# Elementwise work of GpSimd given to the vector and scalar engines, and the S5 chunk scan as a first-order scan in a rotating frame, in a hybrid encoder layer

## The chip, the cores and the metric

The kernel runs on one core of a Trainium2 chip. The metric is the device time of one execution in microseconds (us). The kernel before takes 930.8 us (median of 3 runs, 930.01 to 931.61).

Five engines work side by side, each on its own queue in program order: PE (TensorE, matmuls), DVE (VectorE), ACT (ScalarE), POOL (GpSimd) and SP (SyncE, which issues most of the DMAs). PEld is the loading of weights into PE. An instruction that waits holds up everything behind it in its own queue.

## What is computed

The reference is one layer of a sequence model: 512 positions, 1024 channels, float32. An RMS norm, one input projection, four causal mixers side by side, a gated merge, an output projection, a squared-ReLU MLP and a final norm.

```python
h = _rmsnorm(x, norm1_g)
proj = h @ w_in
p_gdn, p_lru, p_s5, p_rwkv, p_gate = _split(proj, (...))
ys = (_gdn_mixer(p_gdn, ...), _rglru_mixer(p_lru, ...), _s5_mixer(p_s5, ...), _rwkv7_mixer(p_rwkv, ...))
for i in range(N_BRANCH):
    term = jax.nn.sigmoid(gate_logits[:, :, i]) * (ys[i] @ w_branch[i])
    merged = term if merged is None else merged + term
x = x + merged @ w_out
x = x + jnp.square(jax.nn.relu(_rmsnorm(x, norm2_g) @ mlp_w1)) @ mlp_w2
return _rmsnorm(x, final_norm_g)
```

The S5 mixer is the one whose method is changed. It has 16 groups with 64 complex states each; with `lam_bar = exp(lam * dt)` per group and state it is

```python
bu = jnp.einsum("gpc,bsgc->bsgp", b_bar, ug)
h = _linear_recurrence(lam_bar, bu)          # h_t = lam_bar * h_{t-1} + bu_t
y = jnp.einsum("gcp,bsgp->bsgc", c, h).real + d * ug
```

## The kernel before

**Weights.** All large products go through 134 units of weights, each 128 rows by 1024 columns in float32. `fetch_` (L300) brings a unit in: SP loads `raw`, ACT rounds it to `hi`, DVE takes `lo = raw - hi`. There are two buffers of each (`DEEP = 2`), so unit u needs the buffers of unit u - 2 to be free. `gemm` (L317) multiplies a unit in 24 matmuls of 128x512, three for each of 8 slices: `hi` by the high part of the activation, `hi` by its low part, `lo` by the high part. The third matmul of a unit is therefore the first that needs `lo`.

**Phases.** `norm1` (L389) splits x into `xgh` and `xgl` and takes its rms (`norm_stat`, L325); the projections start before the rms is known, and `nproj` (L402) multiplies it in when it takes a result out of PSUM. 22 units are the mixers' input projections and 32 the gates' (`gate`); the mixers' own work stands between them, up to some 30 units in. Then come the branch products (`branch`, 8 units), the merge (8) and the MLP (`mlp`, L1377, 64 units). The last part is the final norm (L1405).

**S5** works in chunks of 8 positions, 64 chunks. `s5_weights` (L1058) makes `lam_bar` (`er`, `sn`, `cs1`, ...), its powers `pw` and the factors; `s5_a` builds `b8` and `s5_o` builds `c8` and Toeplitz blocks, with two products of 128x2048 and an addition each; `s5_b` gives `H`, each chunk's drive, 128 x (re | im) x 8 groups x 64 chunks; `s5_c` (L1235) carries the state over the chunks: blocks of 8 chunks, complex multiply-adds by powers of `lam_bar^8` (`q8`, `li8`), 22 calls of `cmul_add`, all on GpSimd. Then `H` goes by 4 DMAs to `hs`, PE makes `s5y`, a store and 16 loads (`scy`, issued by ACT) turn it round, two DVE instructions add `d * u`, and the gelu and the `glu` product follow.

**The other mixers.** rwkv and gdn each need a triangular inverse (`tri_inverse`, L425), which passes through DRAM (`scrr`, `scrg`). In rwkv, `hsk`/`hbk` are head sums (`head_stat`, L370), `wl` and `al` lora products, `bkT`, `vT` transposes; in the RG-LRU (`lru`, L1004), `lra` and `lrx` are the gates' products and `tt(G, u, u, i, MUL)` (L1028) is the input `u*i`. `lg` is gdn's logits, `ktT` its transposed keys, `oT` the transposed outputs.

**Order.** The order within each queue is not written out by hand: the steps of `PLAN` (L58) are traced with a priority by level (`LV`, L53) and a scheduler merges them by its own estimates when the kernel is built. So a change of one instruction's engine moves others. SBUF places of temporaries come from `al` (L128), which reads a table made for one order (`PLACE`, L23).

Helpers record most instructions at one line each: L104 matmul, L107 activation, L110 `tt` (a tensor_tensor instruction), L114 and L116 `ts`, L119 `stt` (scalar_tensor_tensor). Names such as `c`, `c1a`, `c1b` in the profile are the SBUF regions, not the temporaries.

## Time and profile before

| | before |
|---|---|
| median of 3 runs | 930.8 us (930.01 to 931.61) |
| the profiled execution's span, first to last instruction | 929.2 us |
| around the span (median less span) | 1.6 us |
| busy: PE, DVE, ACT, POOL | 891.0, 517.2, 336.1, 214.7 us |
| instructions: PE, DVE, ACT, POOL | 5267, 854, 453, 229 |
| mean granted clock of PE | 0.978 |
| DMA traffic | 99.52 MB, mean 107 GB/s |

The profile lists every instruction with start, duration and, in brackets, how long its engine had been idle before and what released it. An instruction that is held while it executes, not before, shows no idle time but a long duration. The clock column is the share of full speed that PE was granted. In a row such as `70.77 0.80 PE L104 MATMUL acc<-c,lo ...` the first number is the start in us from the span's begin, the second the duration of the group; `x2` says how many instructions are in it.

### The profile page before, as it was taken

How to read it: one execution, taken by the hardware profiler on the slowest of the kernel's cores; microseconds unless marked ns; L12 is line 12 of the kernel's file. 1: busy time of each engine (PE TensorE's matmuls, PEld its weight loads, DVE VectorE, ACT ScalarE, POOL GpSimd, SP SyncE). 2: the span in 40 equal slices, each digit the busy share in tenths (PEclk: the TensorE clock that was granted, in tenths of full speed). 3: DMA queues.
4: the chain of work that ended last, by engine and by line, in shares of the span. 5: the costliest groups of instructions: out<-in, count | busy, mean ns of one | idle time of the engine just before them, and what ended most of it. 6: DMA issues, size and time to landing. Idle time of an engine off the chain costs nothing.

```text
span 929.2 us, 13124 instructions
## 1 busy us (share of the span) xinstructions
PE 891.0 (96%) x5267; PEld 715.0 (77%) x5267; DVE 517.2 (56%) x854; ACT 336.1 (36%) x453; POOL 214.7 (23%) x229
## 2 busy tenths in 40 slices
...
GB/s 250 180 47 78 113 49 96 115 104 105 182 161 162 172 111 152 68 92 69 90 91 91 98 107 91 91 91 95 110 91 91 99 105 91 91 107 97 80 80 90
DMA packets 73675, 99.52 MB, mean 107 GB/s; under 512 B 41920, under 2 KB 48768, under 8 KB 73600
## 3 DMA queue, kind: packets, MB, share of 16 engines
...
HBM read 85.44 MB, written 11.08 MB: 104 GB/s over the span
## 4 chain that ended last, share of the span: by engine, by line
PE 84%; DVE 5%; POOL 5%; ACT 3%; issue 1%; DMA 1%; ACTq 0%; SPq 0%; DVEq 0%; POOLq 0%
PE acc L104 26%; PE facc L104 19%; PE dacc L104 19%; PE bacc L104 5%; PE oacc L104 5%; POOL c L110 4%; DVE c L119 2%; PE oT L104 2%; ACT c L107 1%; DVE c L110 1%; POOL c1a L110 1%; PE s5y L104 1%; DVE lo L110 1%; DVE c L1194 1%; ACT L107 1%
## 5 line engine op out<-in xcount | busy, mean ns | idle before, releaser
L104 PE MATMUL acc<-c,hi 128*128 128x512 f32 x864 | 288.7, 409 | 5.0 <-DVE c L119 3.6
L107 ACT ACTIVATE hi<-raw 128x1024 fp32r<-128x1024 f32 x134 | 142.1, 1060 | 401.7 <-issue 157.5
L110 POOL TENSOR_TENSOR c<-c 128x512 f32<-128x512 f32 (+4 forms) x86 | 117.7, 1377 | 430.0 <-ACT c1a L107 240.2
L104 PEld LDWEIGHTS acc<-c,hi 128*128 128x128 f32 x864 | 164.9, 193 | 48.7 <-DVE c L119 7.1
L110 DVE TENSOR_TENSOR lo<-raw,hi 128x1024 fp32r<-128x1024 f32 x134 | 173.1, 1292 | 49.8 <-ACT hi L107 49.1
L104 PE MATMUL acc<-c,lo 128*128 128x512 f32 x432 | 174.2, 404 | 7.1 <-DVE lo L110 7.1
L104 PE MATMUL facc<-c,hi 128*128 128x512 f32 x512 | 157.7, 389 | 0.0
L104 PEld LDWEIGHTS facc<-c,hi 128*128 128x128 f32 x512 | 96.1, 188 | 19.9
L104 PEld LDWEIGHTS acc<-c,lo 128*128 128x128 f32 x432 | 83.6, 193 | 26.1 <-DVE lo L110 7.8
L104 PE MATMUL facc<-c,lo 128*128 128x512 f32 x256 | 99.8, 390 | 0.0
L104 PE MATMUL dacc<-c1a,hi 128*128 128x512 f32 x256 | 99.6, 389 | 0.0
L104 PE MATMUL dacc<-c1b,hi 128*128 128x512 f32 x256 | 98.9, 389 | 0.0
L104 PE MATMUL dacc<-c1a,lo 128*128 128x512 f32 x256 | 98.9, 389 | 0.0
L110 DVE TENSOR_TENSOR c<-dacc,c 128x512 f32<-128x512 f32 x32 | 22.1, 692 | 97.0 <-PE dacc L104 96.5
L107 ACT ACT_TABLE_LOAD x40 | 51.3, 1283 | 17.2 <-issue 5.9
L104 PEld LDWEIGHTS dacc<-c1a,hi 128*128 128x128 f32 x256 | 48.0, 188 | 10.1
L104 PEld LDWEIGHTS facc<-c,lo 128*128 128x128 f32 x256 | 48.1, 188 | 10.0
L104 PEld LDWEIGHTS dacc<-c1b,hi 128*128 128x128 f32 x256 | 48.1, 188 | 9.9
L104 PEld LDWEIGHTS dacc<-c1a,lo 128*128 128x128 f32 x256 | 48.0, 188 | 9.9
L119 DVE SCALAR_TENSOR_TENSOR c<-facc,c 128x512 f32<-128x512 f32 x32 | 21.9, 691 | 54.1 <-PE facc L104 50.9
L107 ACT ACTIVATE c<-c 128x512 f32<-128x512 f32 (+3 forms) x71 | 39.8, 572 | 25.7 <-DVE c L110 9.9
L110 DVE TENSOR_TENSOR c<-acc,c 128x512 f32<-128x512 f32 x27 | 18.6, 689 | 45.7 <-PE acc L104 45.6
...
## 6 DMA issues: line engine op xcount, KB each, us to landing
raw<-in_wall_dram SPq DMA_DIRECT2D x134, 512.0 KB, 3.5
...
```

The costliest lines, as they stand in the source:

```text
L104: P.matmul(out=o, lhsT=l, rhs=r, start=start, stop=stop)
L107: A.activation(out=o, in_=i, func=f, scale=scale, bias=bias)
L110: e.tensor_tensor(out=o, in0=a, in1=b, op=op)
L119: V.scalar_tensor_tensor(out=o, in0=a, scalar=s, in1=b, op0=op0, op1=op1)
L1194: V.tensor_copy(out=q8[64 * e:64 * e + 64, :, 0], in_=pw[64 * e:64 * e + 64, :, 8, e:16:2])
```

## The change

Every GpSimd instruction that reads SBUF goes to another engine; GpSimd keeps its fills. To DVE go: the additions of the norms' squares, products in rwkv's first part (`ea`, `af`, `rf`) and an addition in its last, lru's `u*i`, six of gdn's products and sums (`gr`, `br`, `kx`, `kd`) and one addition in `gdn_c`, the 128x2048 products and additions of `s5_a` and `s5_o`, the 24 merge additions of `branch`, and three products at the end. To ACT go: four squares of the first norm, rwkv's `rb` scaling, gdn's `ksq` squares and some copies. In the MLP ACT squares the ReLU in place and rounds it in a second pass, where ACT had squared and rounded in one and GpSimd had squared again.

The chunk scan of S5 is done in polar form. With `lam_bar^8 = a e^(i w)`, `s5_weights` makes a, cos w and sin w by three squarings and a correction of the length; `s5_o` makes tables `ct`, `st` of cos(w n) and sin(w n) for the 64 chunks by doubling, and `am`, the decay a with 0 at each group's first chunk. `s5_c` turns `H` back by w n, runs a real first-order scan with decay `am` on DVE for the real and the imaginary part (512 wide each, the zeros in `am` part the groups), and turns it forward again. The place table is replaced by one that goes by the temporaries' names (`HOME`).

```diff
-PLACE = [(a, int(b)) for a, b in (e.split(":") for e in """
-    c2:47 c0:0 c0:128 c3:204 c3:64 c3:48 c3:272 c3:244 c3:375 c3:533 c1b:91 c3:202 c1a:94 c3:550 c3:64 c1b:110
...
+HOME = {n: [(a[:a.index(":")], int(a[a.index(":") + 1:])) for a in v.split(",")] for n, v in (e.split("=") for e in """
+    xt0=c1b:0 xgh=c0:0 xgl=c0:128 sqa0=c3:650 sqa1=c3:64 sqa2=c3:333 sqa3=c3:618 sqa4=c3:558 sqa5=c1a:81 sqa6=c3:634
...
-    def norm_stat(xt, nm, first=V, parts=1):
-        """1 / rms of xt over the channels, on all partitions; the sum over the tiles in two parts or one."""
+    def norm_stat(xt, nm, parts=1):
             sq = t2(f"sq{nm}{k}")
-            if k < 4 and first is G:
-                tt(G, sq, xt[k], xt[k], MUL)
-            else:
-                act(sq, xt[k], ACT.Square)
-            if k == 0 or k == 7 or k == 4 and first is G:
+            act(sq, xt[k], ACT.Square)
+            if k == 0 or k == 7:
                 accs.append(sq)
             else:
-                tt(first if k < 4 else V, accs[-1], accs[-1], sq, ADD)
+                tt(V, accs[-1], accs[-1], sq, ADD)
                 fr(sq)
...
-            tt(G, ea, ei, af, MUL)
+            tt(V, ea, ei, af, MUL)
-            tt(G, af, af, kf, MUL)
+            tt(V, af, af, kf, MUL)
-            tt(G, rf, rf, kp, MUL)
+            tt(V, rf, rf, kp, MUL)
-            tt(G, of_, of_, bons[m], ADD)
+            tt(V, of_, of_, bons[m], ADD)
...
-        tt(G, v3(gr, 16), v3(gr, 16), neg, ADD)
-        tt(G, v3(gr, 16), v3(gr, 16), s16(gc).rearrange("p (x o) -> p x o", o=1).to_broadcast([128, 16, 64]), SUB)
+        tt(V, v3(gr, 16), v3(gr, 16), neg, ADD)
+        tt(V, v3(gr, 16), v3(gr, 16), s16(gc).rearrange("p (x o) -> p x o", o=1).to_broadcast([128, 16, 64]), SUB)
-        tt(G, v3(br, 16), v3(br, 16), mgs, MUL)
-        tt(G, br, br, gr, MUL)
+        tt(V, v3(br, 16), v3(br, 16), mgs, MUL)
+        tt(V, br, br, gr, MUL)
-        tt(G, v3(kx, 16), v3(ktok, 16), tb(8), MUL)
-        tt(G, v3(kd, 16), v3(ktok, 16), tb(7), MUL)
+        tt(V, v3(kx, 16), v3(ktok, 16), tb(8), MUL)
+        tt(V, v3(kd, 16), v3(ktok, 16), tb(7), MUL)
-            tt(G, u, u, i, MUL)
+            tt(V, u, u, i, MUL)
...
+    def square(c, s, t, u):
+        tt(V, t, c, c, MUL)
+        tt(V, u, s, s, MUL)
+        stt(s, s, 2.0, c, MUL, MUL)
+        tt(V, c, t, u, SUB)
...
+        V.tensor_copy(out=pol[:, 0], in_=s(er))
+        ts(V, pol[:, 1], s(cs1), 1.0, ADD)
+        V.tensor_copy(out=pol[:, 2], in_=s(sn))
+        for _ in range(3):
+            square(pol[:, 1], pol[:, 2], s(t0), s(u1))
+            tt(V, pol[:, 0], pol[:, 0], pol[:, 0], MUL)
+        tt(V, s(t0), pol[:, 1], pol[:, 1], MUL)
+        tt(V, s(u1), pol[:, 2], pol[:, 2], MUL)
+        tt(V, s(t0), s(t0), s(u1), ADD)
+        ts(V, s(t0), s(t0), -0.5, MUL, 1.5, ADD)
+        tt(V, pol[:, 1], pol[:, 1], s(t0), MUL)
+        tt(V, pol[:, 2], pol[:, 2], s(t0), MUL)
...
-        tt(G, q4(b8), cc(bs), pwr(0, 1), MUL)
+        tt(V, q4(b8), cc(bs), pwr(0, 1), MUL)
         tt(V, q4(tm), cc(bx), pwr(1, 1), MUL)
-        tt(G, b8, b8, tm, ADD)
+        tt(V, b8, b8, tm, ADD)
...
-        tt(G, q4(c8), cc(c1), pwr(0, 0), MUL)
+        tt(V, q4(c8), cc(c1), pwr(0, 0), MUL)
         tt(V, q4(tm), cc(c2), pwr(1, 0), MUL)
-        tt(G, c8, c8, tm, ADD)
+        tt(V, c8, c8, tm, ADD)
...
-        # powers 1..8 of lambda_bar^8, rows (g parity, state); li8 holds -im, +im
-        q8_, li8_ = al("s5q", 128), al("s5qn", 128)
-        q8, li8 = v4(q8_, 2, 8), v4(li8_, 2, 8)
-        tq = sm_.tile([128, 2, 8], F, name="s5tq")
+        fr(tm)
+        ct, st, am = t2("s5ct"), t2("s5st"), t2("s5am")
+        ct3, st3, am3 = v3(ct, 8), v3(st, 8), v3(am, 8)
+        pol = S5["pol"]
+        ph_ = al("s5ph", 32)
+        ph = v3(ph_, 4)
         for e in range(2):
-            V.tensor_copy(out=q8[64 * e:64 * e + 64, :, 0], in_=pw[64 * e:64 * e + 64, :, 8, e:16:2])
-        for j in range(1, 8):
-            a = (j + 1) // 2
-            b = j + 1 - a
...
-            tt(V, q8[:, 1, j], tq[:, 0], tq[:, 1], ADD)
-        ts(V, li8[:, 0], q8[:, 1], -1.0, MUL)
-        V.tensor_copy(out=li8[:, 1], in_=q8[:, 1])
-        fr(tm, *S5["tmps"])
-        S5.update(t8w=t8w, c8=c8, q8=q8, li8=li8, q8_=q8_, li8_=li8_)
+            V.tensor_copy(out=ph[64 * e:64 * e + 64, 0:3], in_=pol[64 * e:64 * e + 64, 0:3, e:16:2])
+        V.tensor_copy(out=am3, in_=bcn(ph[:, 0], 64))
+        V.memset(am3[:, :, 0:1], 0.0)
+        V.memset(ct3[:, :, 0:1], 1.0)
+        V.memset(st3[:, :, 0:1], 0.0)
+        tb_ = t2("s5tb")
+        for k in range(6):
+            n = 1 << k
+            u = tb_[:, 0:8 * n].rearrange("p (g n) -> p g n", g=8)
+            v = tb_[:, 256:256 + 8 * n].rearrange("p (g n) -> p g n", g=8)
+            c, s_ = bcn(ph[:, 1], n), bcn(ph[:, 2], n)
+            lo_, up_ = slice(0, n), slice(n, 2 * n)
+            tt(V, u, st3[:, :, lo_], s_, MUL)
+            tt(V, v, ct3[:, :, lo_], s_, MUL)
+            tt(V, ct3[:, :, up_], ct3[:, :, lo_], c, MUL)
+            tt(V, st3[:, :, up_], st3[:, :, lo_], c, MUL)
+            tt(V, ct3[:, :, up_], ct3[:, :, up_], u, SUB)
+            tt(V, st3[:, :, up_], st3[:, :, up_], v, ADD)
+            if k < 5:
+                square(ph[:, 1], ph[:, 2], ph[:, 3], ph[:, 0])
+        fr(tb_, ph_)
+        fr(*S5["tmps"])
+        S5.update(t8w=t8w, c8=c8, ct=ct, st=st, am=am)
...
+    def bcn(ap, n):
+        return ap.rearrange("p (g o) -> p g o", o=1).to_broadcast([128, 8, n])
...
-        q8, li8, H = (S5[n] for n in ("q8", "li8", "H"))
+        ct, st, am, H = (S5[n] for n in ("ct", "st", "am", "H"))
         S5.update({n + "3": v3(S5[t], 16) for n, t in (("t8", "t8w"), ("c8", "c8"), ("ug", "ug"))})
         S5["upv"] = S5["up"].rearrange("p (m t n) -> p m t n", m=2, t=8)
-        H5 = H.rearrange("p (r g b j) -> p r g b j", r=2, g=8, b=8)
-        tA, tB = t1("s5a"), t1("s5b")
-        def cmul_add(dst, src, j, acc, n):
-            a = tA[:, 0:16 * n].rearrange("p (r g b) -> p r g b", r=2, g=8)
-            b = tB[:, 0:16 * n].rearrange("p (r g b) -> p r g b", r=2, g=8)
-            re = q8[:, 0, j].rearrange("p (r g b) -> p r g b", r=1, b=1).to_broadcast([128, 2, 8, n])
-            tt(G, a, src, re, MUL)
+        ta_, tb_ = t4("s5a"), t4("s5b")
+        ct2 = ct.rearrange("p (o n) -> p o n", o=1).to_broadcast([128, 2, 512])
+        for to in range(2):
+            tt(V, v3(ta_, 2), v3(H, 2), ct2, MUL)
             for r in range(2):
-                im = li8[:, r, j].rearrange("p (g b) -> p g b", b=1).to_broadcast([128, 8, n])
-                tt(G, b[:, r], src[:, 1 - r], im, MUL)
-            tt(G, a, a, b, ADD)
-            tt(G, dst, acc, a, ADD)
-        for j in range(1, 8):
-            cmul_add(H5[:, :, :, :, j], H5[:, :, :, :, j - 1], 0, H5[:, :, :, :, j], 8)
-        cr_ = al("s5cr", 128)
-        cr = v4(cr_, 2, 8)
-        G.memset(cr[:, :, :, 0], 0.0)
-        for b in range(7):
-            cmul_add(cr[:, :, :, b + 1:b + 2], cr[:, :, :, b:b + 1], 7, H5[:, :, :, b, 7:8], 1)
-        for j in range(8):
-            cmul_add(H5[:, :, :, :, j], cr, j, H5[:, :, :, :, j], 8)
-        fr(tA, tB, cr_, S5["q8_"], S5["li8_"])
+                tt(V, tb_[:, 512 * r:512 * r + 512], H[:, 512 - 512 * r:1024 - 512 * r], st, MUL)
+            for r in range(2):
+                sl = slice(512 * r, 512 * r + 512)
+                tt(V, H[:, sl], ta_[:, sl], tb_[:, sl], SUB if r != to else ADD)
+                if not to:
+                    V.tensor_tensor_scan(out=H[:, sl], data0=am, data1=H[:, sl], initial=0.0, op0=MUL, op1=ADD)
+        fr(ta_, tb_, ct, st, am)
...
-                tt(G, mg[m], mg[m], gt, ADD)
+                tt(V, mg[m], mg[m], gt, ADD)
...
-                act(dh[:, m, :], r, ACT.Square)
-                tt(G, r, r, r, MUL)
+                act(r, r, ACT.Square)
+                act(dh[:, m, :], r, ACT.Copy)
...
-                tt(G, hs[k], hs[k], rs, MUL)
+                tt(V, hs[k], hs[k], rs, MUL)
```

How this moves instructions, in the queues as built (before has lines some 7 lower than after, from L104 on):

At the start of the program DVE's queue before held the low parts of x (`c0<-c2,pr,c0`, stt) and few additions of squares (`c3<-c3`), since GpSimd did the other ones:

```order
L110 TENSOR_TENSOR lo0_180<-raw0_181,hi0_183 128x1024
L119 SCALAR_TENSOR_TENSOR c0_75<-c2_78,pr_81,c0_75 128x512 x6
L110 TENSOR_TENSOR c3_79<-c3_79 128x512
L119 SCALAR_TENSOR_TENSOR c0_75<-c2_78,pr_81,c0_75 128x512
L110 TENSOR_TENSOR c3_79<-c3_79 128x512
L119 SCALAR_TENSOR_TENSOR c0_75<-c2_78,pr_81,c0_75 128x512
L116 TENSOR_SCALAR omu_176<-pr_81 128x8
```

and now every addition of squares stands between the low parts; this is the end of the stretch:

```order
L126 SCALAR_TENSOR_TENSOR c0_75<-c1b_77,pr_81,c0_75 128x512
L117 TENSOR_TENSOR c3_79<-c3_79 128x512
L126 SCALAR_TENSOR_TENSOR c0_75<-c1b_77,pr_81,c0_75 128x512
L117 TENSOR_TENSOR c3_79<-c3_79 128x512
L126 SCALAR_TENSOR_TENSOR c0_75<-c1b_77,pr_81,c0_75 128x512
L123 TENSOR_SCALAR omu_176<-pr_81 128x8
L123 TENSOR_SCALAR omu_176<-pr_81 128x2
L117 TENSOR_TENSOR c3_79<-pr_81 128x16
L117 TENSOR_TENSOR c3_79<-c3_79,c1a_76 128x512
L126 SCALAR_TENSOR_TENSOR c0_75<-c1b_77,pr_81,c0_75 128x512
L117 TENSOR_TENSOR c3_79<-c3_79 128x512
L126 SCALAR_TENSOR_TENSOR c0_75<-c1b_77,pr_81,c0_75 128x512
```

The low part of the last tile of x, for which unit 0's last matmuls wait, now has six additions ahead of it in DVE's queue, where two were; the narrow rows are other steps' constants.

DVE's queue around `lo7`, before. `c3<-c2,c1a 128x2048` is one of s5's products, the two copies at L1194 and `s5tq` belong to s5's `c8` and powers, `hstk` and the copy at L378 to rwkv's head norm, on which PE's `hbk` waits:

```order
L110 TENSOR_TENSOR c1a_76<-acc_421,c3_79 128x512
L110 TENSOR_TENSOR c3_79<-c2_78,c1a_76 128x2048
L1194 COPY c3_79<-c1a_76 64x2x8 x2
L110 TENSOR_TENSOR lo7_520<-raw7_521,hi7_523 128x1024
L119 SCALAR_TENSOR_TENSOR c3_79<-c1a_76,pr_81,c3_79 128x511
L110 TENSOR_TENSOR s5tq_1237<-c3_79 128x8 x2
L114 TENSOR_SCALAR hstk_305<-hsk_300 128x8
L110 TENSOR_TENSOR c2_78<-c3_79,c1a_76 128x8x64
L110 TENSOR_TENSOR c3_79<-s5tq_1237 128x8
L547 RECIPROCAL hstk_305<-hstk_305 128x8
L110 TENSOR_TENSOR s5tq_1237<-c3_79 128x8 x2
L378 COPY c1a_76<-hstk_305 128x512
```

and now, one unit on, around `lo8`:

```order
L117 TENSOR_TENSOR c1b_77<-acc_476,c3_79 128x512
L117 TENSOR_TENSOR c3_79<-c2_78,c1a_76 128x2048
L117 TENSOR_TENSOR c1a_76<-c3_79 128x16
L117 TENSOR_TENSOR lo8_711<-raw8_712,hi8_714 128x1024
L126 SCALAR_TENSOR_TENSOR c3_79<-c1b_77,pr_81,c3_79 128x511
L117 TENSOR_TENSOR c3_79<-c1a_76 128x16 x2
L117 TENSOR_TENSOR c3_79<-c1a_76 128x2048
L117 TENSOR_TENSOR c1a_76<-c3_79 128x16
L117 TENSOR_TENSOR c3_79<-acc_519,c3_79 128x512
L117 TENSOR_TENSOR lo9_744<-raw9_745,hi9_747 128x1024
L117 TENSOR_TENSOR c3_79<-c2_78,c1a_76 128x2048
```

Three instructions of 128x2048 stand here, where one did, and the rows of `s5tq` are gone.

Around the loads of s5's output (`scy`), ACT's queue before:

```order
L1283 COPY c3_79<-s5y_1597 128x512
L502 COPY c2_78<-z3pr_1864 32x16x32
L1292 DMA c3_79<-scy_1615 16x8x64 x2
L107 ACTIVATE hi24_2508<-raw24_2506 128x1024
L1292 DMA c3_79<-scy_1615 16x8x64 x7
L107 ACTIVATE hi25_2543<-raw25_2541 128x1024
L1292 DMA c3_79<-scy_1615 16x8x64 x6
L686 COPY c3_79<-oT_2662 128x2x64
L1292 DMA c3_79<-scy_1615 16x8x64
L829 DMA c1a_76<-gscr_1978 64x16x64 x2
```

and now:

```order
L1320 DMA c3_79<-scy_1555 16x8x64 x4
L669 COPY c3_79<-c3_79 64x256
L1320 DMA c3_79<-scy_1555 16x8x64 x6
L688 COPY c3_79<-oT_2602 128x2x64
L1320 DMA c3_79<-scy_1555 16x8x64 x6
L114 ACTIVATE hi28_3061<-raw28_3059 128x1024
L114 ACTIVATE c1b_77<-c1b_77 128x512
L114 ACT_TABLE_LOAD
L114 ACTIVATE c3_79<-c3_79 128x1024
```

DVE's queue at the two stt that add `d * u` to these loads (`c3<-c1a,pr,c3`, L119 before and L126 now), before:

```order
L119 SCALAR_TENSOR_TENSOR c3_79<-c1a_76,pr_81,c3_79 128x512
L110 TENSOR_TENSOR lo25_2540<-raw25_2541,hi25_2543 128x1024
L110 TENSOR_TENSOR c2_78<-vtT_2014,c2_78 64x256 x2
L110 TENSOR_TENSOR c3_79<-sn_2655,c3_79 64x256
L110 TENSOR_TENSOR c3_79<-c3_79,wc_251 64x256
L119 SCALAR_TENSOR_TENSOR c3_79<-c1a_76,pr_81,c3_79 128x512
```

and now:

```order
L126 SCALAR_TENSOR_TENSOR c3_79<-c1a_76,pr_81,c3_79 128x512
L668 COPY c1b_77<-r1_2612 64x256
L117 TENSOR_TENSOR c1b_77<-acc_2513,c3_79 128x512
L126 SCALAR_TENSOR_TENSOR c3_79<-c1a_76,pr_81,c3_79 128x512
L117 TENSOR_TENSOR lo28_3058<-raw28_3059,hi28_3061 128x1024
```

Before, `hi24` and `hi25` stood between the loads, and `lo25` between the two stt; now all 16 loads and both stt stand ahead of `hi28` and `lo28`. The scan itself left GpSimd's queue, which went from 153 rows to 17.

More of the change, by code (lines that the diff above doesn't have):

```diff
@@ L47 @@
+""".split())}
 NU = 134
@@ L119, in stt @@
         V.scalar_tensor_tensor(out=o, in0=a, scalar=s, in1=b, op0=op0, op1=op1)
-    regions, live, clock, live_names = {}, {}, [0], []
+    regions, live, clock, turns = {}, {}, [0], {}
     def region(name, n, dt=F):
@@ L130, in al @@
         g = -(-n // GRAN)
-        k = len(live_names)
-        live_names.append(name)
-        if k < len(PLACE):
-            r, o = PLACE[k]
-        else:
+        k = turns[name] = turns.get(name, -1) + 1
+        r, o = HOME[name][k] if k < len(HOME.get(name, ())) else (None, 0)
+        if r is None or regions[r][3] is not dt or regions[r][1][o:o + g].any():
             best = None
@@ L329, in norm_stat @@
             sq = t2(f"sq{nm}{k}")
-            if k < 4 and first is G:
-                tt(G, sq, xt[k], xt[k], MUL)
-            else:
-                act(sq, xt[k], ACT.Square)
-            if k == 0 or k == 7 or k == 4 and first is G:
+            act(sq, xt[k], ACT.Square)
+            if k == 0 or k == 7:
                 accs.append(sq)
             else:
-                tt(first if k < 4 else V, accs[-1], accs[-1], sq, ADD)
+                tt(V, accs[-1], accs[-1], sq, ADD)
                 fr(sq)
@@ L392, in norm1 @@
             split_g(xs[k], "g1", k, xgh[:, k, :], xgl[:, k, :])
-        N1["rs"] = norm_stat(xs, "a", G)
+        N1["rs"] = norm_stat(xs, "a")
         fr(xt)
```

73 lines of the change are left out of this document (38 added, 35 removed).

## The prediction

> **What bounds the kernel now.** I read the busy shares of the page first, then the windows, then the waits of TensorE and what stands in front of them on the other engines. A line of the page, and the windows (columns: stretch in us, its length, busy time of PE, PEld, DVE, ACT and POOL with counts, granted clock, DMA share, GB/s):
>
> ```profile
> PE 891.0 (96%) x5267; PEld 715.0 (77%) x5267; DVE 517.2 (56%) x854; ACT 336.1 (36%) x453; POOL 214.7 (23%) x229
> 63.10:72.50 9.40, 2.33 (x7) 1.52 (x6) 9.36 (x4) 0.56 (x1) 9.40 (x4) 0.64 0.08 22
> 72.50:79.40 6.90, 2.91 (x7) 1.72 (x6) 6.90 (x4) 0.00 (x0) 6.77 (x2) 0.75 0.12 47
> 79.40:86.20 6.80, 5.33 (x14) 4.22 (x15) 6.66 (x27) 0.72 (x1) 0.00 (x0) 0.50 0.12 36
> 86.20:174.40 88.20, 87.50 (x490) 66.52 (x489) 67.30 (x171) 43.76 (x58) 49.62 (x104) 1.00 0.32 93
> 174.40:185.20 10.80, 5.78 (x19) 4.59 (x18) 5.72 (x7) 10.20 (x14) 5.61 (x12) 0.68 0.60 127
> 230.00:913.00 683.00, 682.91 (x3827) 554.75 (x3826) 335.57 (x450) 215.95 (x284) 108.88 (x76) 1.00 0.32 105
> 492.48 21.76 PE acc L104 x96
> ```
>
> TensorE is the bound, and from 230 to 913 us it never stops (682.91 of 683). There 96 matmuls take 21.76 us, 0.2267 each, so a unit of 24 takes 5.44. The matmuls stay the same, so only time in which TensorE waits or runs at a lower clock can be won: before 230 us and after 913. In order of time:
>
> ```profile
> 21.62 0.73 PE L104 MATMUL acc<-c,hi 128*128 128x512 f32 x2 [0.45 <-ACT hi L107]
> 70.77 0.80 PE L104 MATMUL acc<-c,lo 128*128 128x512 f32 x1 [7.07 <-DVE lo L110]
> 80.87 1.11 PE L381 MATMUL hbk<-cs,c1a 128*128 128x128 f32 x4 [5.46 <-DVE c1a L378]
> 179.84 1.97 PE L641 MATMUL bkT<-cs,c 128*128 128x128 f32 x8 [5.02 <-ACT c L642]
> 181.45 1.20 PE L104 MATMUL acc<-c,hi 128*128 128x512 f32 x2
> 185.01 0.49 PE L104 MATMUL acc<-c,lo 128*128 128x512 f32 x1
> 213.00 0.69 PE L799 MATMUL ktT<-cs,c 128*128 128x128 f32 x2 [2.39 <-ACT c L800]
> 213.34 0.78 PE L104 MATMUL acc<-c,lo 128*128 128x512 f32 x1
> 216.00 0.40 PE L104 MATMUL acc<-c,lo 128*128 128x512 f32 x1
> ```
>
> A wait costs twice, since the matmuls behind it run at half clock (0.50 in 79.40:86.20). At unit 7, 63 to 86 us: waits 7.07 + 5.46 = 12.5, and matmuls at half rate from 70.8 to 75.4 and from 80.9 to 86.2, 9.9 us where 5.0 do: **17.5**. At 174.4: 5.02, and the eight matmuls from 181.45 to 185.01 take 3.56 for 1.81: **6.8**. At 210.6: 2.39, and six matmuls from 213.34 to 216.00 take 2.66 for 1.36: **3.7**.
>
> **The first part, 63 to 86 us.** Who holds `lo7` and the head-norm row `hbk`? DVE and POOL there:
>
> ```profile
> 62.17 7.46 POOL L110 TENSOR_TENSOR c<-c 128x512 f32<-128x512 f32 x3 [4.67 <-ACT c L107]
> 62.73 5.72 DVE L1194 COPY c<-c1a 64x16 f32<-64x16 f32 x2
> 68.48 2.24 DVE L110 TENSOR_TENSOR lo<-raw,hi 128x1024 fp32r<-128x1024 f32 x1
> 69.60 4.84 POOL L110 TENSOR_TENSOR c<-c1a 128x2048 f32<-128x2048 f32 x1
> 70.64 4.35 DVE L119 SCALAR_TENSOR_TENSOR c<-c1a,pr,c 128x511 f32<-128x511 f32 x1
> 74.52 4.83 POOL L110 TENSOR_TENSOR c<-c 128x2048 f32<-128x2048 f32 x1
> 74.91 4.53 DVE L110 TENSOR_TENSOR s5tq<-c 128x8 f32<-128x8 f32 x2
> ```
>
> A DVE instruction with both inputs in SBUF ends when POOL's does: the stt at 74.99, POOL's first of 2048 at 74.44; the pair of `s5tq`, which is 8 elements wide, at 79.44, POOL's second at 79.35. PE reaches `lo7` and `hbk` behind them. The same forms where POOL reads nothing:
>
> ```profile
> 28.32 1.23 DVE L110 TENSOR_TENSOR lo<-raw,hi 128x1024 fp32r<-128x1024 f32 x1
> 47.76 2.28 DVE L110 TENSOR_TENSOR c<-c,c1a 128x2048 f32<-128x2048 f32 x1
> 49.97 1.21 DVE L560 TENSOR_TENSOR_SCAN c1b<-c1a,c1b 128x512 f32<-128x512 f32 x1
> 57.54 0.74 DVE L119 SCALAR_TENSOR_TENSOR c1b<-c,pr,c1a 128x512 f32<-128x512 f32 x1
> 58.20 0.68 DVE L110 TENSOR_TENSOR c1b<-c,c1a 128x512 f32<-128x512 f32 x1
> ```
>
> The next row starts 0.08 before such a row ends (57.54 + 0.74 against 58.20), so an stt (two inputs and a column) of 512 costs 0.66, a tt (two inputs) of 512 0.60, one of 2048 2.20, a scan 1.13, a `lo` 1.15. The four DVE rows of the stretch took 5.72 + 2.24 + 4.35 + 4.53 = 16.8 where 1.15 + 0.66 and, for four small ones, under 1 would do: 14 us of DVE's delay there are POOL's reads.
>
> After the change POOL only fills memory, so nothing stretches; but what POOL did comes into DVE's queue, and whether the 17.5 go is decided by DVE's own work. Between `lo2` and `lo10`, counted in the new order: 8 `lo` 9.1; 5 tt of 2048 (two before: s5's b8 and c8 have moved) 11.1; 18 tt of 512 (fifteen before) 10.8; 11 stt and 2 scans 9.5; 256-wide ones and a copy 3.1; some 130 narrow ones 15.0 (estimate, 0.08 to 0.2 each, as most wait for the one ahead). That is **58.6 us**, for 50.4 before with the stretching on top. TensorE's products between the same units are 60.7: 8 x 5.44 = 43.5, and 17.2 of transposes, head sums and loras. By the start-up below `lo2` ends some 4 us before unit 2 asks for it (estimate), so it fits, barely: the 17.5 go, but I give back **4**. The loras `al` and `wl` now stand in unit 3, behind stt rows that DVE reaches only then, and `lo5` is ready about 3 us before it is due. Bounds: 0, if DVE finds every input ready; 8, if it loses its leads and waits of 4 open, with as much at half clock behind them.
>
> **The scan.** POOL's chunk scan (49.62 us of POOL in 86.20:174.40) held lru's `u*i` and with it ScalarE, which gave the wait of 5.02:
>
> ```profile
> 174.57 0.72 ACT L107 ACTIVATE c<-c1b,cl 128x512 f32<-128x512 f32 x1 [5.54 <-POOL c L110]
> ```
>
> In DVE's queue the scan is 2 tt of 1024 (1.15 each, as `lo`), 8 of 512 at 0.60 and 2 scans at 1.13: 9.4 us for POOL's 50. Its tables `ct` and `st` are six doublings of 6 tt, 36 tt with 6 x 504 elements in all, and 20 narrow ones for the squares (some 9 us, estimate), in place of 42 narrow ones (some 5); the polar form is 24 narrow ones, 3 to 4. With this and with lru's and gdn's products DVE has 49.4 us between `lo17` and `lo25`, TensorE 56.1 in the same units. `u*i` is now two of 512 on DVE, 0.60 each, not behind a scan. What is late next is ScalarE: its table loads and the round trips of the triangular inverse through DRAM stay. I count 6.8 and 3.7 as gone and give back **2** (0 to 4).
>
> **Start and end.** POOL squares and adds for the first norm, and DVE is stretched beside it:
>
> ```profile
> 6.06 1.72 DVE L110 TENSOR_TENSOR lo<-raw,hi 128x1024 fp32r<-128x1024 f32 x1 [4.47 <-ACT hi L107]
> 7.70 8.57 DVE L119 SCALAR_TENSOR_TENSOR c<-c,pr,c 128x512 fp32r<-128x512 f32 x6
> 5.66 9.29 POOL L110 TENSOR_TENSOR c<-c 128x512 f32<-128x512 f32 x6 [1.89 <-DMA c<-in_xT_dram]
> 19.18 0.74 DVE L119 SCALAR_TENSOR_TENSOR c<-c,pr,c 128x512 fp32r<-128x512 f32 x1
> ```
>
> The last split of x ends at 19.84. After: 6.06 + 1.14 + 8 x 0.66 + 6 x 0.60 + 0.4 of small ones = 16.5, so unit 0 ends 3.4 earlier, and the matmul at 21.62 with it: **3.4** (2 to 4.5: ScalarE now has a square beside each split, and x must have landed). At the end:
>
> ```profile
> 918.19 6.51 DVE L119 SCALAR_TENSOR_TENSOR c<-c,pr 128x512 f32<-128x512 f32 x5 [1.72 <-ACT c L362]
> 918.23 4.60 POOL L110 TENSOR_TENSOR c<-c 128x512 f32<-128x512 f32 x3 [45.21 <-ACT c L362]
> ```
>
> Alone DVE needs 3 x 0.60 + 5 x 0.66 = 5.1: **1.4**. The 24 merge adds (24 x 0.60 = 14.4 us), gdn's products, and the MLP's second pass on ScalarE lie behind 230 us, where DVE is busy for 335.57 of 683 us and ScalarE for 215.95, under matmuls that never stop: nothing. Without that cover the adds alone would cost 14.4.
>
> **A new wait.** In the new order ScalarE's `hi28` stands behind all 16 loads of s5's output (`scy`), and DVE's `lo28` behind the two stt that need them. Rows of these today:
>
> ```profile
> scy<-c SPq DMA_DIRECT2D x1, 512.0 KB, 3.9
> c<-scy ACTq DMA_DIRECT2D x16, 32.0 KB, 3.3
> 239.77 3.33 ACTq L1292 DMA_DIRECT2D c<-scy  x6
> 248.64 0.75 DVE L119 SCALAR_TENSOR_TENSOR c<-c1a,pr,c 128x512 f32<-128x512 f32 x1 [3.01 <-DMA c<-scy]
> ```
>
> Today `lo25` stands ahead of the second stt, and its wait of 3.01 hurts nobody. After, the last `s5y` product ends 18.5 us of TensorE work before unit 28. From there: the copy and the store 0.6 + 3.9; 16 issues at 3.33 / 6 = 0.55, 8.9; landing 3.3; two stt and `lo28` 2.5: 19.2, and one copy in the middle of the issues waits for TensorE's `oT`, 2 more. `glu` right behind needs the gelu of the same stt, 1 to 2 later. So a wait of 2 or 3 us opens; with half clock I take **3** (0, if the store starts early; 6, if the waits of `lo28` and `glu` add up).
>
> **Sum**, on the median of 930.8 (span 929.2, so 1.6 around it): won 3.4 + 17.5 + 6.8 + 3.7 + 1.4 = 32.8; given back 4 + 2 + 3 = 9; net 23.8: **907.0**.
>
> The Trainium skill, "TensorE: Matmul & The Clock Gate", section What's actually happening, has the clock fall after an idle window of about 3.4 us. Here a wait of 2.39 was already followed by half clock; were it as the page says, give-backs under 3.4 would cost only themselves and the sum would be some 904.5.
>
> **Rivals.** (a) Nothing is given back: 898.0. For it: DVE's sums are below TensorE's in both stretches; against: leads of 3 us in a queue that waits for ScalarE and TensorE in between. (b) DVE becomes the bound of units 3 to 10 and again at 17 to 28: give-backs at their upper ends 8 + 4 + 6 = 18 give 916, and one more stall with half clock, as at 179.84, 922. For it: 58.6 against 60.7. (c) The stall only moves: all that TensorE doesn't lose at POOL it loses at DVE, which has more work than before; 930.8. The Trainium skill, "Perfetto Trace Analysis", section Identifying the Most-Contended Engine, would work on the busiest engine first, here PE at 96%, which this change leaves as it is; but 891.0 busy counts the matmuls at half clock. (d) Slower: `lo` comes late in each of units 4 to 10. If a wait opens each, the unit's 5.44 us run at half clock: 5 us or so a unit with the wait, 7 units 35 us, less the 32.8 won and with the 2 of the later stretch: 935. It decides if DVE's 58.6 become over 64.7 (60.7 and its lead of 4), 10% more than these rows give, or 6 us of its own waits; against it: DVE at the same place today waits for little else than POOL.
>
> **Numbers.** Forecast, 902 to 914: 0.56; (a) to 902: 0.13; (b) 0.22; (c) 0.04; (d) 0.05. The range, 898 to 920, takes in all give-backs' bounds and most of (b). A measurement of this kernel tells about 0.2% (1.9 us) from no change: faster 0.91, same 0.04, slower 0.05.
>
> **What would show it.** Right: clock 1.00 from 60 to 90 us with no wait over 1 us at unit 7; DVE's `lo` at 1.2 throughout; no ScalarE wait for POOL; a wait at unit 28 with `lo` or `glu`. Wrong: DVE at 9 tenths and over with waits <-DVE lo in units 3 to 10 (b, d); the 5.02 back under the name of DVE.

## The result and the profile after

| | before | after |
|---|---|---|
| median of 4 runs | 931.2 us (930.01 to 932.73) | 909.7 us (906.51 to 910.78) |
| ratio | | 0.977 (95% interval 0.975 to 0.979) |
| span of the profiled execution | 929.2 us | 904.7 us |
| mean granted clock of PE | 0.978 | 0.993 |

The kernel became 21.5 us faster by the medians and 24.5 by the two profiled executions (after's is the fastest of its four); 23.8 had been forecast, and 907.0 lies 2.7 under the median. From the page of after:

```profile
span 904.7 us, 12969 instructions
PE 881.8 (97%) x5267; PEld 708.8 (78%) x5267; DVE 521.0 (58%) x958; ACT 367.8 (41%) x507; POOL 3.3 (0%) x13
```

DVE took over most of GpSimd's 214.7 us and is busy for only 3.8 more than before (517.2), though it has 104 more instructions: before, some of its busy time was being held. The windows of after (stretch, length, busy time of PE, PEld, DVE, ACT, POOL, clock, DMA share, GB/s):

```profile
60.00:72.50 12.50, 12.50 (x62) 9.03 (x61) 12.44 (x16) 7.30 (x9) 0.00 (x0) 1.00 0.26 84
72.50:90.00 17.50, 17.42 (x89) 14.01 (x88) 17.45 (x24) 7.14 (x10) 0.00 (x0) 1.00 0.33 99
174.40:185.20 10.80, 10.80 (x169) 8.86 (x168) 10.80 (x25) 8.66 (x10) 0.13 (x1) 1.00 0.34 121
198.50:207.00 8.50, 5.87 (x49) 4.82 (x40) 0.83 (x2) 1.59 (x5) 0.00 (x0) 0.60 0.60 150
230.00:890.00 660.00, 656.11 (x3702) 532.73 (x3701) 329.14 (x459) 227.81 (x310) 0.00 (x0) 1.00 0.32 102
```

PE works through the stretch at 60 to 90 us at full clock, where it had lost 17.5 us, and through 174 to 185. DVE is busy there from end to end (17.45 of 17.50) and still in time. New is the fourth line: 2.6 us without work at 198.5, and a clock of 0.60. PE's waits in after (released by, us in total, times, longest):

```profile
PE t1pr L111 <- issue: 2.6, 1, 2.6
PE acc L111 <- DVE c L126: 2.5, 6, 0.8
PE acc L111 <- DVE lo L117: 2.2, 3, 1.0
PE glu L111 <- ACT c L114: 1.3, 1, 1.3
```

The waits of 7.07, 5.46, 5.02 and 2.39 us are all gone. DVE's rows in the stretch where before a `lo` had lasted 2.24 and an stt of 511 columns 4.35:

```profile
68.16 1.22 DVE L117 TENSOR_TENSOR lo<-raw,hi 128x1024 fp32r<-128x1024 f32 x1
72.62 0.73 DVE L126 SCALAR_TENSOR_TENSOR c1b<-c,pr,c1b 128x511 f32<-128x511 f32 x1
75.47 0.75 DVE L126 SCALAR_TENSOR_TENSOR c1b<-c1a,pr,c 128x512 f32<-128x512 f32 x1
```

To set stage against stage I add up what PE loses: over all neighbouring matmul records the distance of their starts, less the distance that such a pair has at full clock (the tenth percentile over like pairs). It holds waits and half clock together. A stage lies up to 20 us earlier after than before, and how the pairs are grouped moves what a stage won by up to 2 us, so single lines are rough. The tail is counted from DVE's first row behind the last norm to the end of the span.

| PE's loss, us | before | after | won | forecast |
|---|---|---|---|---|
| 0 to 25 | 11.9 | 7.6 | 4.3 | 3.4 |
| 25 to 60 | 2.5 | 2.9 | -0.4 | 0 |
| 60 to 120 | 22.0 | 5.3 | 16.7 | 17.5 - 4 |
| 120 to 222 | 21.4 | 15.3 | 6.2 | 10.5 - 2 |
| 222 to 300 | 7.1 | 10.4 | -3.2 | -3 |
| 300 to 870 | 16.6 | 18.4 | -1.8 | 0 |
| tail | 11.0 | 8.6 | 2.4 | 1.4 |

The lines add up to 24.2 of the 24.5.

### The profile page after: what moved, and what is told of

Read it like the earlier page. It is cut to its first block, busy times and chain, and to the rows that moved or that the text cites. A ratio compares the mean times of both kernels' runs of the same rounds, so it can differ in the third digit from the quotient of the medians.

```text
span 904.7 us, 12969 instructions
## 1 busy us (share of the span) xinstructions
PE 881.8 (97%) x5267; PEld 708.8 (78%) x5267; DVE 521.0 (58%) x958; ACT 367.8 (41%) x507; POOL 3.3 (0%) x13
## 4 chain that ended last, share of the span: by engine, by line
PE 77%; DVE 11%; ACT 4%; DMA 4%; issue 2%; SPq 1%; ACTq 1%; DVEq 0%
PE acc L111 20%; PE facc L111 19%; PE dacc L111 19%; PE oacc L111 5%; PE bacc L111 4%; DVE c L117 4%; DVE lo L117 2%; ACT c L114 2%; PE oT L111 1%; DMA c1a<-gscr 1%; ACT L114 1%; DVE c L126 1%; PE s L111 1%; DMA raw<-in_wall_dram 1%; DVE c1a L117 1%
## 5 line engine op out<-in xcount | busy, mean ns | idle before, releaser
L111 PE MATMUL acc<-c,hi 128*128 128x512 f32 x864 | 277.6, 399 | 4.0 <-DVE c L126 2.5
L117 DVE TENSOR_TENSOR lo<-raw,hi 128x1024 fp32r<-128x1024 f32 x134 | 163.8, 1223 | 43.3 <-ACT hi L114 43.2
L111 PE MATMUL dacc<-c,hi 128*128 128x512 f32 x256 | 99.3, 389 | 0.0
L114 ACT ACTIVATE c<-c 128x512 f32<-128x512 f32 (+4 forms) x118 | 69.4, 593 | 28.1 <-DVE c L117 20.6
L126 DVE SCALAR_TENSOR_TENSOR c<-facc,c 128x512 f32<-128x512 f32 x32 | 22.0, 691 | 82.0 <-PE facc L111 80.1
L111 PEld LDWEIGHTS dacc<-c,hi 128*128 128x128 f32 x256 | 48.1, 188 | 10.1
L117 DVE TENSOR_TENSOR c<-c 128x512 f32<-128x512 f32 (+8 forms) x118 | 50.0, 441 | 7.0 <-ACT c L114 5.0
L111 PE MATMUL dacc<-c1a,hi 128*128 128x512 f32 x128 | 49.6, 389 | 0.0
L111 PE MATMUL dacc<-c1b,hi 128*128 128x512 f32 x128 | 49.6, 389 | 0.0
L111 PE MATMUL dacc<-c,lo 128*128 128x512 f32 x128 | 49.5, 389 | 0.0
L111 PE MATMUL bacc<-c1a,hi 128*128 128x512 f32 x128 | 41.0, 402 | 0.1
```

What stands on the lines that cost most here:

```text
L111: P.matmul(out=o, lhsT=l, rhs=r, start=start, stop=stop)
L114: A.activation(out=o, in_=i, func=f, scale=scale, bias=bias)
L117: e.tensor_tensor(out=o, in0=a, in1=b, op=op)
L126: V.scalar_tensor_tensor(out=o, in0=a, scalar=s, in1=b, op0=op0, op1=op1)
```

## The experiments

My theory: a GpSimd instruction that reads SBUF holds DVE's instructions of two SBUF inputs, and before lost its time so. Rivals: it lost the time to waiting for GpSimd's results, or to the order of the queues that came with them.

### Free order: four kernels

The first four edits were made in the changed kernel and the scheduler merged the queues anew.

**Reads alone.** Behind the making of c8, near 84 us, twelve products on GpSimd whose results nothing uses:

```diff
+        for i in range(12):
+            j = 512 * (i % 4)
+            tt(G, dm, c8[:, j:j + 512], c8[:, j:j + 512], MUL)
```

> The changed kernel with 12 more GpSimd products of 128x512 that read c8 as soon as DVE has made it (some 68 us in) and write to a place that nobody reads. Theory (GpSimd's SBUF reads hold DVE): DVE rows of two SBUF inputs beside them grow from 0.7 to over 1.3 us, lo over 1.8; DVE's lead there is some 6 to 10 us, so TensorE waits behind it, and the time goes from 909.7 up by 3 to 12, to 913-922. Rival (before, DVE and TensorE waited for GpSimd's results and for the place in the queue, not for its reads): nobody waits for these products, 909.7 within 2, and DVE's rows keep their lengths.

Measured: 926.9 (ratio to before 0.994, interval 0.991 to 0.997), over what I expected. Beside them DVE's `lo` lasted 1.95 and 1.46 us and a product of 512 1.52. But PE lost only 3.6 us more than in after between 60 and 120 us; its long waits stood a hundred us further on:

```profile
PE ktT L801 <- ACT c L802: 6.0, 1, 6.0
PE vtT L872 <- DVE c L823: 3.0, 1, 3.0
```

**Fills alone.** In the same place 24 fills and one product of 16 columns.

```diff
+        for i in range(24):
+            G.memset(dm, 0.0)
```

> The control of the run with reads: at the same place 24 GpSimd fills of 128x512 into that spare place, which read nothing (one product of 16 columns ahead of them ties them to the same moment). Theory: DVE's rows keep their lengths, 909.7 within 2. If any GpSimd work beside DVE costs, or if the new rows only shuffle the scheduler's order to something worse, it grows like the run with reads.

Measured: 914.0 (ratio 0.979, interval 0.976 to 0.981). Rows of GpSimd and of DVE beside them:

```profile
83.72 14.28 POOL L1205 MEMSET c<- 128x512 f32 x24
85.52 1.17 DVE L117 TENSOR_TENSOR lo<-raw,hi 128x1024 fp32r<-128x1024 f32 x1
```

The `lo` keeps its length beside the fills. The 4.3 us over after came with a wait of 4.5 for `ktT`, again far from the edit, which points to the order.

**S5's four wide instructions** (128x2048, for b8 and c8) back on GpSimd.

```diff
-        tt(V, q4(b8), cc(bs), pwr(0, 1), MUL)
+        tt(G, q4(b8), cc(bs), pwr(0, 1), MUL)
-        tt(V, b8, b8, tm, ADD)
+        tt(G, b8, b8, tm, ADD)
```

and the same two for c8.

> The changed kernel with s5's four 128x2048 products and additions back on GpSimd, the rest as changed. DVE has 8.8 us less work before unit 10. Theory: two thirds of the stretch is theirs; DVE rows beside them last to their ends again, and 8 to 18 of the 17.5 us won at 63-86 us come back: 918-928. Rival (the new order of the queues did it, or DVE's load decides): 905-911.

Measured: 926.1 (ratio 0.992, interval 0.989 to 0.995), with waits for `hsk` (4.6) and `lo` (4.4) where the edit is, and for `us` (2.5) and `s5y` (2.0) far from it.

**The old chunk scan** on GpSimd with its powers `q8`, all else as changed.

```diff
-        ta_, tb_ = t4("s5a"), t4("s5b")
...
-                    V.tensor_tensor_scan(out=H[:, sl], data0=am, data1=H[:, sl], initial=0.0, op0=MUL, op1=ADD)
...
+        for j in range(1, 8):
+            cmul_add(H5[:, :, :, :, j], H5[:, :, :, :, j - 1], 0, H5[:, :, :, :, j], 8)
```

> The changed kernel with the old chunk scan (powers q8, li8 and cmul_add on GpSimd), everything else off GpSimd as changed. Theory: the scan alone held what cost 6.8 us at 174 us and part of 3.7 at 210; with u*i on DVE lru no longer stands behind it, so only its reads beside DVE and the later hs remain: 910-917. If the full 6.8 comes from the scan itself, 916 or more; rival (the scan on DVE is only a longer DVE queue and its place is the t1pr wait of 2.6 at 198 us): 905-909.

Measured: 932.4 (ratio 0.999, interval 0.998 to 1.001), far over what I expected. GpSimd is busy for 50 us, and between 200 and 225 us the clock is 0.73; but `t1pr` starts at 239 us, where after has it at 194, and the longest wait is for a `hi`. So much was reordered that the scan's own share can't be read from it. A version of this kernel in a fixed order was not run, so what the polar form of the scan is worth by itself stays open.

The first three say that GpSimd's reads stretch DVE's rows and its fills don't, and the four together that a new order alone moves the time by several us. For the rest, neighbours in each engine's queue were tied to the order that they have in the changed kernel (a dependency without a semaphore), so that an edit moves nothing else.

### Tied order: control

```diff
+    for j in sorted(range(len(ins)), key=rank.get):
+        i = ins[j]
+        if i.engine in last:
+            tc.add_manual_dep(i, last[i.engine], info, reason="pin")
+        last[i.engine] = i.name
```

> The changed kernel as it is, with each engine's instructions tied to the order that they have in it, so that later edits move nothing else. Nothing is computed differently. If the tie costs nothing: 908 to 911, as the changed kernel. If ties between neighbours of one queue cost time: over 911.

Measured: 910.0 (905.53 to 914.11), ratio 0.977 (0.973 to 0.982). The tie costs nothing. It is the base of all that follows.

### Start

```diff
-            act(sq, xt[k], ACT.Square)
+            if k < 4 and nm == "a":
+                tt(G, sq, xt[k], xt[k], MUL)
+            else:
+                act(sq, xt[k], ACT.Square)
...
-                tt(V, accs[-1], accs[-1], sq, ADD)
+                tt(G if k < 4 and nm == "a" else V, accs[-1], accs[-1], sq, ADD)
```

> Order tied. Of the first norm, four squares and the three additions of them go back to GpSimd. Theory (reads hold DVE): the low parts of x end 3.4 to 4.3 us later, 912.5 to 914.5, and DVE's rows in the first 20 us grow from 0.66 to over 1.2. Rival (the start is set by x landing or by ScalarE): 908.5 to 911.

Measured: 914.1, 4.1 over the control (ratio 0.981, 0.977 to 0.986); PE's loss up to 25 us is 13.1 for 8.0. Rows of this kernel:

```profile
7.15 4.47 POOL L117 TENSOR_TENSOR c<-c1b 128x512 f32<-128x512 f32 x3 [0.40 <-DMA c1b<-in_xT_dram]
7.76 7.80 DVE L126 SCALAR_TENSOR_TENSOR c<-c1b,pr,c 128x512 fp32r<-128x512 f32 x5
```

Five instructions take 1.56 each in place of 0.66. The term of the start is confirmed in kind, and in size as far as 4.1 us can be told from runs of one kernel that lie 5 to 9 us apart.

### S5's products again, in tied order

The edit is that of the third kernel above.

> Order tied. The four instructions of 128x2048 for s5's b8 and c8 go back to GpSimd. Theory (GpSimd's reads of SBUF hold DVE): each takes 4.4 to 4.9 on GpSimd, DVE's rows of two inputs beside them last as long as they do, lo comes late in units 3 to 10, and 7 to 17 us come back: 917 to 927. Rival (only the place in the queues counted, and DVE has 8.8 us less to do): 906 to 911, no row of DVE longer than in the changed kernel.

Measured: 918.8, 8.8 over the control (ratio 0.987, 0.983 to 0.992). In the profiled execution, the slowest of its four (924.2), PE loses 14.9 between 60 and 120 us where the control loses 5.7. The way from GpSimd to PE, in the order of its links:

```profile
73.33 5.40 POOL L117 TENSOR_TENSOR c<-c 128x2048 f32<-128x2048 f32 x1 [5.00 <-issue]
74.25 5.03 DVE L126 SCALAR_TENSOR_TENSOR c1b<-c,pr,c1b 128x511 f32<-128x511 f32 x1
79.21 4.36 DVE L126 SCALAR_TENSOR_TENSOR c1b<-c1a,pr,c 128x512 f32<-128x512 f32 x1
83.50 4.98 DVE L117 TENSOR_TENSOR c1b<-c 128x512 f32<-128x512 f32 x1
89.84 0.81 ACT L114 ACTIVATE c1b<-c1b,omu,pr 128x512 f32<-128x512 f32 x1 [12.60 <-DVE c L117]
91.17 1.12 PE L1191 MATMUL b8T<-cs,c 128*128 128x128 f32 x4 [9.41 <-ACT c L1192]
```

Three instructions of DVE take 14.4 us for 2.2; ACT waits 12.60 for the last of them, and PE 9.41 for ACT's next. No engine on this way waits for a result of GpSimd, and none of the waits' names says GpSimd: it shows only in durations.

### Reads that nobody waits for

Three products of 128x2048 behind the making of c8, on 64 partitions, their results unused; then the same as twelve of 512 columns.

```diff
+        for i in range(3):
+            j = 2048 * (i % 1)
+            tt(G, tm[64:128, j:j + 2048], c8[64:128, j:j + 2048], c8[64:128, j:j + 2048], MUL)
...
```

```diff
+        for i in range(12):
+            j = 512 * (i % 4)
+            tt(G, tm[64:128, j:j + 512], c8[64:128, j:j + 512], c8[64:128, j:j + 512], MUL)
...
```

> Order tied. GpSimd gets three products of 128x2048 (64 partitions) behind the making of c8, near 85 us, whose results nothing uses. Theory (a GpSimd instruction that reads SBUF holds a DVE instruction of two SBUF inputs until it ends): DVE rows of two inputs beside them last 3 to 5 us, one for each of the three, lo for the unit near 88 us comes 2 to 6 us late, half clock behind it, 913 to 920. Rival (before lost its 12.5 us to waiting for GpSimd's results, not to its reads): nothing waits for these, so 908.5 to 911.5.

> Order tied. The same products as twelve of 128x512 (64 partitions): the same bytes, each instruction a quarter as long. Theory (held until the instruction ends): rows of DVE beside them grow by 1.5 us at most, two or three of them ahead of lo, 910 to 914, less than with the three long ones by 2 or more. Rival (what counts is the bytes that GpSimd reads): as with the long ones within 1 us.

Measured, long: 919.3 (912.08 to 923.37; ratio 0.985, 0.980 to 0.990); short: 912.0 (909.63 to 918.99; ratio 0.980, 0.975 to 0.984). Rows of the long ones:

```profile
85.79 12.15 POOL L117 TENSOR_TENSOR c<-c 64x2048 f32<-64x2048 f32 x3 [82.37 <-DVE c L117]
86.90 3.04 DVE L117 TENSOR_TENSOR c<-c1b,c1a 128x512 f32<-128x512 f32 x1
89.86 4.62 DVE L117 TENSOR_TENSOR lo<-raw,hi 128x1024 fp32r<-128x1024 f32 x1
94.52 3.97 DVE L117 TENSOR_TENSOR c<-c,c1b 128x512 f32<-128x512 f32 x1
```

and its wait of PE:

```profile
PE acc L111 <- DVE lo L117: 7.6, 4, 5.4
```

Rows of the short ones:

```profile
85.59 17.14 POOL L117 TENSOR_TENSOR c<-c 64x512 f32<-64x512 f32 x12 [82.17 <-DVE c L117]
87.44 1.20 DVE L117 TENSOR_TENSOR lo<-raw,hi 128x1024 fp32r<-128x1024 f32 x1
90.56 1.93 DVE L117 TENSOR_TENSOR lo<-raw,hi 128x1024 fp32r<-128x1024 f32 x1
```

One row of DVE is held for each long one. Taken singly, GpSimd's three last 3.60, 3.93 and 4.46 us and end at 89.39, 93.39 and 97.94; DVE's rows end at 89.94, 94.48 and 98.49, that is 0.55, 1.09 and 0.55 later, which is about what each takes alone (0.60, 1.15, 0.60). So DVE waited for the end of GpSimd's instruction and then ran at its own speed. It goes the other way too: the second of the short ones lasted 3.62 us, the others 1.04 to 2.02, beside three rows of DVE with two SBUF inputs that kept their lengths, the `lo` of 1.20 among them.

So the reads are enough, without a result that is waited for; and for the same elements the length of one instruction decides how long a row of DVE is held (4.62 or 1.93 for a `lo`). What that is worth in time is looser. The long ones cost 9.3 us over the control by the medians, the short ones 2.0, and the intervals of the two touch. The profiled executions are not typical: that of the long ones took 912.1, the fastest of its four, that of the short ones 919.0, the slowest of its four. Between 60 and 120 us PE loses some 7 us more than in the control with the long ones and 5 with the short ones, so the rows do not bear out a gap of 7.

The Trainium skill, "SBUF — State Buffer", section SBUF: two separate sides, calls the pair of ports that the two engines share an exclusive lock, held for the whole instruction, where DVE has two SBUF inputs and GpSimd reads SBUF. The rows above agree on each point: held to the end (4.62 for 1.20), with reads, not with fills (1.17). Two SBUF inputs are not the only case here: in before, the second of two copies of 64x16, with one input (5.72 us for the two), lasted 4.44 us beside a GpSimd product of 2048 columns and ended with it.

### Merge and end

```diff
-                tt(V, mg[m], mg[m], gt, ADD)
+                tt(G, mg[m], mg[m], gt, ADD)
...
-                tt(V, hs[k], hs[k], rs, MUL)
+                tt(G, hs[k], hs[k], rs, MUL)
```

> Order tied. The 24 additions of the merge and the last three products go back to GpSimd. Theory: the additions lie under matmuls that never stop and cost nothing, the last products stretch DVE's last rows from 0.66 to about 1.3 us and cost 1.4 to 2.4: 911 to 912.5, the tail behind the last norm's wait 9.9 to 11 us long where it is 8.6. Rival (the additions matter too, bacc waits for them): over 913, with waits of PE <- POOL or of DVE behind them between 320 and 500 us.

Measured: 910.7 (ratio 0.977, 0.974 to 0.979), a little under what I expected. The end:

```profile
898.76 6.51 DVE L126 SCALAR_TENSOR_TENSOR c<-c,pr 128x512 f32<-128x512 f32 x5 [1.72 <-ACT c L364]
898.81 4.60 POOL L117 TENSOR_TENSOR c<-c 128x512 f32<-128x512 f32 x3 [396.50 <-ACT c L364]
```

These are the durations of before to the hundredth, and the tail is 10.4 long for 8.6. The 24 additions cost nothing: between 300 and 500 us PE loses 15.5 here, 15.8 in after.

### The new wait of t1pr

In after PE stands still in the middle of a run of like matmuls, with nothing that the profile names:

```profile
198.46 0.21 PE L111 MATMUL t1pr<-c1b,c 32*32 32x16 f32 x3
201.30 0.26 PE L111 MATMUL t1pr<-c,c1b 32*16 32x16 f32 x8 [2.63 <-issue]
```

My first theory was a place in SBUF. The decay table `s5am` shares columns with rwkv's inverse matrix, whose loads from DRAM therefore wait for the last S5 scan.

```diff
-    s5am=c2:18 s5ph=c2:175 s5tb=c3:282 ...
+    s5am=c3:282 s5ph=c2:175 s5tb=c3:282 ...
...
-        fr(tb_, ph_)
+        fr(tb_)
+        am = t2("s5am")
+        am3 = v3(am, 8)
+        V.tensor_copy(out=am3, in_=bcn(ph[:, 0], 64))
+        V.memset(am3[:, :, 0:1], 0.0)
+        fr(ph_)
```

> Order tied. The decay table of the S5 scan (s5am) gets another place in SBUF, and is built after the turning tables; nothing else changes. Theory: the 2.6 us wait of t1pr near 200 us, and the half clock behind it, come from the place that s5am shares with rwkv's inverse matrix, whose loads have to wait for the last scan. Then this wait goes, the clock in 200 to 208 us stays at 0.9 or more, and the time is 904 to 906.5. Rival: t1pr waits for the data's way through DRAM or for ScalarE's queue, which this edit leaves: 908.5 to 911, wait still over 2.

Measured: 912.0 (ratio 0.979, 0.976 to 0.983), the wait still there. In this kernel:

```profile
187.75 1.38 ACTq L455 DMA_DIRECT2D c<-scrr  x2
202.97 0.25 PE L111 MATMUL t1pr<-c,c1b 32*16 32x16 f32 x8 [3.12 <-issue]
```

The loads go out at 187.75, where after has them at 190.16 and the control at 190.95; PE waits as before. The theory fell. What stays the same is the place: in after and in all seven tied kernels that keep PE's order (control, start, products, both reads, merge, place) PE stops behind the 173rd of the 192 matmuls of `t1pr`, though that matmul runs at anything from 198.5 to 209.1 us. The 174th is of the same form as many before it. The transfers of instructions, from the page of after, and then from its transfers between 198.5 and 199 us:

```profile
q8 instruction: 41, 0.67, 0.3%
```

```profile
q8 instruction: 1, 0.02, 14.0%
```

41 transfers of 16 KB for 5267 matmuls make one block for 128 matmuls, each with its weight load. In after none goes between 177 and 198.5 us, while 255 matmuls run, two blocks. The one behind 198.5 comes as PE stops; from 196.9 to 198.7 us 167 matmuls had run, more than a block.

So the second theory: the burst uses up its block before the next is there. To spread it, 17 large matmuls of the same unit, six from ahead of the burst and eleven from behind it, were put between its small ones.

```diff
-PE: t1pr x3, acc x11, t1pr x93, s5y x2, acc x11
+PE: t1pr x3, acc x5, (t1pr x5 or x6, acc) x17, s5y x2
```

(counted in instructions; one of `t1pr` is two matmuls, one of `acc` is one).

> Order tied, with one place changed: the burst of 186 small matmuls of t1pr near 197 us gets 17 matmuls of the same unit of weights spread between its own, which stood ahead of it and behind it. Theory: the wait of t1pr, always behind the same matmul, is PE running out of instructions: the next block of 16 KB of them is fetched too late when 128 matmuls pass in 1.4 us. Spread over some 6 us they leave the fetch its time: the wait falls under 1 us, the clock in 200 to 208 us stays over 0.9, and the time is 904 to 907. Rival (t1pr waits for data, by an edge that the profile doesn't show): the wait of 2 to 3 us stays at the same matmul, 909 to 912.

Measured: 910.5 (903.84 to 914.18; ratio 0.976, 0.971 to 0.981). The wait is gone and the clock full where it stood, but another stretch is at half clock:

```profile
196.00:208.00 12.00, 12.00 (x211) 7.49 (x211) 1.63 (x3) 0.73 (x3) 0.00 (x0) 1.00 0.63 158
298.00:307.00 9.00, 9.00 (x75) 7.04 (x73) 0.91 (x3) 1.51 (x4) 0.00 (x0) 0.62 0.35 115
```

And the spread pays for itself with as much, as two rows of the large ones with eleven or so small ones between show:

```profile
202.10 0.50 PE L111 MATMUL acc<-c,hi 128*128 128x512 f32 x1
202.75 0.50 PE L111 MATMUL acc<-c,lo 128*128 128x512 f32 x1
```

They start 0.65 apart. A large one at full clock takes 0.227 and eleven small ones 0.12 (1.8 us for 167), so each round of the two costs 0.3 more than its matmuls, and 17 rounds 5. From the first `t1pr` to the first `z2pr`, the same work, it is 15.3 us here, 14.7 in the control and 15.5 in after. That the wait hangs on how thick the instructions come is shown, and that it isn't data.

That it falls at the end of a block shows in two of the kernels of free order, whose queues of PE differ. The only waits of over 1 us that the profile of each puts down to `issue`:

```profile
243.49 0.22 PE L111 MATMUL t1pr<-c,c1b 32*16 32x16 f32 x3 [2.69 <-issue]
315.72 0.25 PE L111 MATMUL t1pg<-c,c1a 32*16 32x16 f32 x8 [1.64 <-issue]
```

The first is from the kernel with the old scan, where `t1pr` stops behind its 157th matmul; the second from the one with the reads alone, where gdn's inverse stops. Counted in records of PE (weight loads, matmuls and semaphores), the stop lies behind record 2497 in all eight kernels above, and behind 2753 and 4545 here: 256 and 8 times 256 further. The 41 blocks for 10604 records are one for 259. Cut at these places into blocks of 256 records, PE's queue takes 24 us for a block at the median. All nine blocks that passed in 1.2 to 1.3 us end in a stop; of the 19 that took 1.9 to 2.5 us, one does. In before the burst of `t1pr` begins 127 records earlier in PE's queue, only one such place lies inside it, and no block passes in under 3.6 us. So the change brought this wait by where it put `t1pr` in the queue.

A gain was not had from the spread. No kernel of these runs beats the changed one by more than its runs scatter.

## Why the prediction was right, step by step

- **The stretch at 60 to 90 us** was the largest term, and its cause was right: held DVE rows, seen in durations. The clock is 1.00 there, `lo` lasts 1.2 throughout, and no wait over 1 us stands at unit 7. Of the 4 us given back 0.8 came (16.7 won of 17.5): DVE's queue, counted at 58.6 us against PE's 60.7, fits as counted, with leads of `lo` down to 0.1 and 0.4 us near 82 and 88. So rival (a) held here, and (b) and (d) did not. The prediction has a held row end with GpSimd's; by the long reads it ends later by its own length.
- **The waits of 5.02 and 2.39** near 174 and 210 went, as forecast. The stretch gave 6.2 and not 8.5 because of a wait that no step named, that of `t1pr`: 2.6 us and the half clock behind it. Two waits for `lo`, of 1.0 and 0.5 near 162 and 188, come on top. The step that failed is the 2 given back for units 17 to 25, which thought of ACT and DRAM, not of PE's own instructions. That the scan ahead of `u*i` caused the wait of 5.02 rests on the rows of before; no run here took it back alone.
- **Unit 28**: forecast 3 with `lo` or `glu`; `glu` waits 1.3 for ACT, and the stretch lost 3.2 with what follows. `lo` was in time there; one at 224.6 came 0.7 late.
- **Start**: 4.3 for 3.4, within its 2 to 4.5; the run that undid it gave 4.1.
- **End**: DVE's rows take 5.2 us, counted as 5.1, in place of 6.5. The rest of the 2.4 is the last store, which takes 3.4 us behind them and took 4.5.
- **Behind 300 us** the moved additions are free, as forecast. 1.8 were lost there that the prediction didn't have; 1.5 are lost near 507 us, where `oacc` waits 0.7 for two roundings `hi`. The MLP's second pass was not taken back by a run.
- **Clock**: by the Trainium skill's window of some 3.4 us, in "TensorE: Matmul & The Clock Gate", section What's actually happening, the sum was 904.5. After the 2.63 of `t1pr` the clock is 0.60 over 8.5 us, so shorter waits cost twice here, and the sum without that rule was the better one.
- **Rival (c)**, that the stall only moves, is out: the largest loss in any stage is 3.2 us, against 29.6 won in the others.
- **The sum** came nearer than its terms. Against the forecast column, 3.2 us more were won at 60 to 120, 0.9 at the start and 1.0 at the end; 2.3 less at 120 to 222, 1.8 behind 300, and 0.6 in the other two. That these nearly cancel (24.2 for 23.8) is luck.
- The Trainium skill, "Perfetto Trace Analysis", section Identifying the Most-Contended Engine, would have the engine with the highest occupancy optimized first, though for TensorE it doesn't take busy time as the measure of what is left. Here PE had the highest before and after (96% and 97%), and the 21.5 us came from moving work of other engines.
